# Modulation rows reordered, gate rows made on TensorE, and one chain for both inverses in a two-layer decoder kernel

## The chip, the cores and the metric

The kernel runs on one core of a Trainium2 chip. The metric is the device time of one execution in microseconds (us). The engines are TensorE (PE, its weight loads PEld), VectorE (DVE), ScalarE (ACT), GpSimd (POOL) and SyncE (SP), whose queue issues nearly all loads, in program order.

## The reference, cut to what matters

One sequence of 256 tokens of width 1024 goes through a first block and then a second block. The change lies in the first part of the first block.

```python
def hybrid_layer(x, c, w_ada, b_ada, ...):
    mods = jax.nn.silu(c) @ w_ada + b_ada
    shift1, scale1, gate1, shift2, scale2, gate2 = jnp.split(mods[:, None, :], 6, axis=-1)
    h = rms_norm(x, norm1_g) * (1.0 + scale1) + shift1
    proj = h @ w_in
    y_rwkv = rwkv7_time_mix(proj[..., :RWKV_PROJ], ...)
    y_moba = moba_attention(proj[..., RWKV_PROJ:], q_norm_g, k_norm_g)
    x = x + gate1 * (jnp.concatenate([y_rwkv, y_moba], axis=-1) @ w_out)
    h = rms_norm(x, norm2_g) * (1.0 + scale2) + shift2
    y = moe_ffn(h.reshape(B * S, D), w_router, b_router, w_gate_up, b_gate_up, w_down, b_down)
    return x + gate2 * y.reshape(B, S, D).astype(x.dtype)

def rwkv7_time_mix(p, ...):
    ...
    def step(state, inp):
        r_t, w_t, k_t, v_t, kk_t, a_t = inp
        sa = jnp.einsum('bhij,bhj->bhi', state, -kk_t)
        state = (state * w_t[:, :, None, :]
                 + sa[..., None] * (kk_t * a_t)[:, :, None, :]
                 + v_t[..., None] * k_t[:, :, None, :])
        y_t = jnp.einsum('bhij,bhj->bhi', state, r_t)
        return state, y_t
    ...
```

`mods` has 6 parts of 1024 columns. `rwkv7_time_mix` has 8 heads of width 64; `moba_attention` is causal attention of 8 heads here, since the sequence is one block long. `moe_ffn` has 32 experts, four for each token. The second block is a stick-breaking attention with 256 memory tokens, and a feed-forward part.

## The kernel before, in words

**Order of work.** Up to about 287 us the kernel makes the modulation, the projections, the time mix, the attention, w_out, and the router. From there to about 1200 us it streams the experts' weights, 6 chunks of 2 MB for each expert. The rest is the second block. Weights come through `stream` (L135, its DMA is L140): each call takes a slot of 2 MB and issues one load on SP. The ring has three slots, and two further places, lent[0] and lent[1], serve the first part as working memory (X and Y) and the experts as slots later. A load waits on SP until its slot is free, and all later loads wait behind it. The order of the instructions on each engine is not written by hand: the framework's scheduler sets it from the program's order and its own estimates.

**Modulation.** w_ada's columns are taken in 12 chunks of 512. `ada_rows` (L279) makes the rows of several chunks in one bank of PSUM: a matmul with the bias (L281), then for each chunk 8 matmuls of 128x512 (L286, 16 records in the trace), which leave four partial sums for each chunk, one in each quarter of the bank's partitions. ScalarE copies the bank (L292), and `ada_col` (L324) turns rows into columns. Chunks 0 and 2, then 1 and 3, are made at the start, chunks 6 to 9 (shift and scale of the second norm) after the attention's projections. The two gates (chunks 4, 5 and 10, 11) are made in `gate_rows` (L298): VectorE multiplies and accumulates in one operation (L306), POOL in two (L308, L310), over 8 pieces of each chunk, and `gate_bc` adds up the partitions and spreads the sum by a matmul with ones.

**Projections.** h is split in two parts, hh and hl, and each piece of a weight into wsh (ScalarE, L147) and wsl (L148, on VectorE, every fourth on POOL); a product is three matmuls. `dense_T` (L397 to L400, "pj") makes the lora's inputs, k, r and v in this order, `dense_N` (L412 to L414, "pn") the attention's q, k and v, which the texts call q, k2 and v2. The lora's second matrices are wua and gup; cb is a table of constants.

**Time mix.** The 256 tokens are two superchunks of 128. `sub` (L541) makes a triangular matrix for each head of a superchunk (lab), and its diagonal blocks of 16x16 (Lc, by lc). `invert` (L558) inverts these blocks in 15 steps: POOL makes a selection (sel, L566), TensorE a row (L567), VectorE multiplies by it and adds (L572, L574). The two superchunks' steps alternate. Then follow the transposes (tr, L660), decays (dc, L655), the masked products Lak, Lrk, Lrb (L671) and `solve` (L696) with Dt (the inverse spread out), f and u on TensorE. The attention's heads (L786 to L820) run between these: `s` is normalized on VectorE (L803). mqs (L601) is the normalized q or k, turned by mt (L609). sc2 and sh2 (L632, L633) are the second norm's scale and shift, with small loads of norm_g (L629) and of the router's weights (L628). prod (L641) is the product of r, k and r_k for the bonus.

Of the kernel before, what the change touches and what calls it, by code (L numbers as in the profile page):

```python
# [121 lines left out]
class Kernel:  # L122
# [132 lines left out]
    def phase1(self):  # L255
# [15 lines left out]
        bada = self.gate2[0:13, 512:1024]  # L271
        nc.sync.dma_start(bada[1:13], A["b_ada"])
# [6 lines left out]
        def ada_rows(cis):  # L279
            ps = self.psum("ada")  # L280
            PE.matmul(ps[0:32, :], ident[0:13, 1:33], bada, start=True, stop=False, skip_group_check=True)  # L281
            for n, i in enumerate(cis):
                w = self.stream(A["w_ada"][:, i * 512:(i + 1) * 512].rearrange("(k p) f -> p k f", p=128), 8, 512)
                for k in range(8):
                    j = k % 4
                    PE.matmul(ps[32 * j:32 * j + 32, :], scw[:, k, 32 - i:64 - i], w[:, k, :],  # L286
                              start=n == 0 and 0 < k < 4, stop=n == len(cis) - 1 and k >= 4, skip_group_check=True)
                if i == 0:
                    nc.sync.dma_start(x1, A["x"].rearrange("(a p) d -> p a d", p=128))
                    self.expert_bias(pxn)  # L290
            r = p1.tile([128, 512], F32, tag="ar", name="ar")
            ACT.activation(r, ps, AF.Copy)  # L292
            return r

        gacc = p1.tile([128, 4, 512], F32, tag="gacc", name="gacc")
        sc = scw[:, :, 32]

        def gate_rows():  # L298

            for q, i in enumerate((4, 5, 10, 11)):  # L300
                w = self.stream(A["w_ada"][:, i * 512:(i + 1) * 512].rearrange("(k p) f -> p k f", p=128), 8, 512)
                o, eng = gacc[:, q], POOL if q % 2 else DVE
                for k in range(8):
                    c = sc[:, k:k + 1]
                    if eng is DVE and k:
                        DVE.scalar_tensor_tensor(o, w[:, k], c, o, op0=OP.mult, op1=OP.add)  # L306
                    else:
                        eng.tensor_scalar(w[:, k] if k else o, w[:, k], c, None, op0=OP.mult)  # L308
                        if k:
                            eng.tensor_tensor(o, w[:, k], o, op=OP.add)  # L310
                r = slice(32 * q, 32 * q + 1)
                eng.tensor_tensor(o[r], o[r], self.gate2[r, 512:1024], op=OP.add)
# [18 lines left out]
        for q, i in enumerate((4, 5, 10, 11)):  # L331
            nc.gpsimd.dma_start(self.gate2[32 * q:32 * q + 1, 512:1024], A["b_ada"][i:i + 1])
# [23 lines left out]
        X, Y = lend(0), lend(1)  # L356
# [116 lines left out]
        self.act_set("natural_log_exp_and_others")  # L473

# [45 lines left out]
        eB, eC = ExitStack(), ExitStack()  # L520
        pb = self.pool("pb", es=eB)
        blk16, e16, idd = self.kb("blk16"), self.kb("e16"), self.kb("idd")
# [17 lines left out]
        def sub(s):  # L540

            tt = slice(s * 128, s * 128 + 128)
            L16 = pb.tile([128, 8, 128], F32, tag="L16", name="L16")
            Lof = pb.tile([128, 8, 128], F32, tag="Lof", name="Lof", bufs=2)
            for p, ps in pairs(aT, bT, tt, "lab"):
                DVE.tensor_tensor(par(L16, p), ps, bc("m16", 4), op=OP.mult)
                DVE.tensor_tensor(par(Lof, p), ps, bc("moff", 4), op=OP.mult)
            Lc = pb.tile([128, 8, 16], F32, tag=f"Lc{s}", name="Lc")
# [3 lines left out]
            ACT.activation(Lc.rearrange("p h q -> p (h q)"), ps[:, 0:128], AF.Copy)  # L552

            Tc = pb.tile([128, 8, 16], F32, tag=f"Tc{s}", name="Tc")
            POOL.tensor_copy(Tc, e16[:, None, :].to_broadcast([128, 8, 16]))
            return Lof, Lc, Tc

        def invert(s, r):  # L558

            Lof, Lc, Tc = parts[s]  # L560
            if r % 4 == 0:
                rows[s] = self.psum("row", chain=True)
                for q in range(r, min(r + 4, 15)):
                    if s == 0:
                        sel[q] = pb.tile([128, 128], F32, tag="sel", name="sel", bufs=5)
                        POOL.tensor_scalar(sel[q], blk16, e16[:, q:q + 1], None, op0=OP.mult)  # L566
                    PE.matmul(rows[s][:, (q % 4) * 128:(q % 4) * 128 + 128], sel[q], Lc.rearrange("p h q -> p (h q)"),  # L567
                              start=True, stop=True, skip_group_check=True)
            n = 15 - r
            t = pb.tile([128, 8, 16], F32, tag=f"tq{s}", name="tq")  # L570
            o = (r % 4) * 128
            DVE.tensor_tensor(t[:, :, 0:n], rows[s][:, o:o + 128].rearrange("p (h q) -> p h q", h=8)[:, :, r + 1:16],  # L572
                              Tc[:, :, r:r + 1].to_broadcast([128, 8, n]), op=OP.mult)
            DVE.tensor_tensor(Tc[:, :, r + 1:16], Tc[:, :, r + 1:16], t[:, :, 0:n], op=OP.add)  # L574

        parts = [sub(s) for s in range(2)]
        parts2, rows, sel = {}, {}, {}
        for r in range(15):
            for s in range(2):
                invert(s, r)  # L580
# [37 lines left out]
        r1 = ada_rows(range(6, 10))  # L618
        gate_rows()
# [20 lines left out]
        for m in range(4):  # L640
            DVE.scalar_tensor_tensor(prod[:, m], rT[:, m], self.v("rk", m), kT[:, m], op0=OP.mult, op1=OP.mult)  # L641
# [54 lines left out]
        def solve(s):  # L696
            Lof, Lc, Tc = parts[s]
# [3 lines left out]
            for hf in range(2):  # L701
                hsl = slice(4 * hf, 4 * hf + 4)
                (POOL if hf else DVE).tensor_tensor(
                    Dt[:, hsl], Tc[:, hsl, None, :].to_broadcast([128, 4, 8, 16]),
                    blk16.rearrange("p (b q) -> p b q", q=16)[:, None].to_broadcast([128, 4, 8, 16]), op=OP.mult)
# [186 lines left out]
        for dst, q in ((gate, 0), (self.gate2, 2)):  # L892
            for h in range(2):
                ACT.activation(dst[:, h * 512:(h + 1) * 512], gate_bc(q + h), AF.Copy)
# [733 lines left out]
```

## Time and profile before

| | |
|---|---|
| runs before, median of 3 | 1540.79 us (1537.72 to 1542.02) |
| the profiled execution | 1538.45 us |
| its span | 1536.7 us |
| TensorE busy | 1405.6 us (91%) |
| VectorE busy | 574.7 us (37%) |
| ScalarE busy | 387.6 us (25%) |
| POOL busy | 200.3 us (13%) |
| DMA of experts' weights on the chain that ended last | 24% of the span |
| granted TensorE clock, mean | 0.982 |

Busy shares are means over three stages with different limits, so what a change in one stage is worth has to be read in that stage. Times in the rows below are counted from the span's start. A row of a timeline shows the start, the length, the engine, the line and the operation, and in brackets how long the engine stood idle before and what ended that. The matmuls' ends are modelled, so that two in a row overlap by a little, and the spacing of their starts is the better measure.

### The profile page before, as it was taken

What the parts mean: (1) busy time and instruction counts of PE and PEld (TensorE: products, weight loads), DVE (VectorE), ACT (ScalarE), POOL (GpSimd) and SP (SyncE); (2) the same over time, 40 slices, a digit from 0 to 9 for tenths busy, and PEclk for the clock granted to TensorE, in tenths of its full rate; (3) what the DMA queues carried; (4) which work ended last, traced back from release to release, by engine and by line L of the source; (5) the groups of instructions that cost most, each with busy time, mean ns of one, the idle gap of its engine ahead of it and who ended that gap; (6) DMA issues with size and microseconds to landing.
All of it is one profiled execution on the core that took longest, in us unless ns stands there. A gap on an engine that the chain in (4) does not pass through costs nothing.

```text
span 1536.7 us, 19084 instructions
## 1 busy us (share of the span) xinstructions
PE 1405.6 (91%) x7818; PEld 805.5 (52%) x7818; DVE 574.7 (37%) x1138; ACT 387.6 (25%) x759; POOL 200.3 (13%) x180
## 2 busy tenths in 40 slices
PE   4999999899999999888988878999988899799997
PEld 1986776443434344233333334443333497599996
DVE  2576886422222222122112122121211446655455
ACT  4872244200100011011001011110100367355552
POOL 1233581000000000000000000000000334212221
PEclk9998999899999999999999999999999999999999
DMA  9833746899999999999999999999999851535440
GB/s 332 277 110 116 272 165 266 345 429 427 426 426 386 427 428 428 428 427 426 428 428 428 426 422 428 428 429 427 426 428 428 334 186 55 219 138 192 178 152 28
DMA packets 74885, 505.15 MB, mean 329 GB/s; under 512 B 5693, under 2 KB 6717, under 8 KB 50313
## 3 DMA queue, kind: packets, MB, share of 16 engines
q1 hardware_dynamic: 74328, 503.22, 80.3%
q8 instruction: 63, 1.03, 0.3%
q10 hardware_dynamic: 288, 0.52, 0.1%
q14 instruction: 30, 0.24, 0.0%
q0 software_dynamic: 176, 0.14, 0.0%
HBM read 502.82 MB, written 1.05 MB: 328 GB/s over the span
## 4 chain that ended last, share of the span: by engine, by line
PE 43%; DMA 24%; DVE 2%; ACT 1%; issue 0%; SPq 0%; DVEq 0%; ACTq 0%
DMA w<-w_gate_up 24%; PE py L116 7%; PE pg L116 6%; PE pu L116 6%; PE d L1302 3%; PE d L1301 3%; PE d L1303 3%; PE ga L116 2%; PE acc L1308 2%; PE acc L1309 2%; PE acc L1310 2%; PE cb L116 2%; ACT at L1169 1%; PE z L1389 0%; PE so L1419 0%
## 5 line engine op out<-in xcount | busy, mean ns | idle before, releaser
L116 PE MATMUL pg<-w,xe 128*64 128x512 f32 x1024 | 270.9, 599 | 43.5 <-DMA w<-w_gate_up 43.0
L116 PE MATMUL pu<-w,xe 128*64 128x512 f32 x1024 | 268.4, 594 | 0.0
L116 PE MATMUL py<-w,at 128*64 128x512 f32 x1024 | 228.9, 599 | 23.8 <-ACT at L1169 20.6
L1158 DVE TENSOR_SCALAR u<-pu 128x512 f32<-128x512 f32 (+1 forms) x33 | 22.2, 675 | 452.5 <-PE pu L116 439.2
L1157 ACT ACTIVATE sg<-pg 128x512 f32<-128x512 f32 (+1 forms) x33 | 19.3, 586 | 669.7 <-PE pg L116 668.0
L116 PEld LDWEIGHTS pg<-w,xe 128*64 128x64 f32 x1024 | 72.1, 137 | 190.2 <-issue 115.8
L116 PEld LDWEIGHTS py<-w,at 128*64 128x64 f32 x1024 | 71.1, 137 | 158.8 <-issue 130.3
L116 PEld LDWEIGHTS pu<-w,xe 128*64 128x64 f32 x1024 | 75.8, 137 | 145.7 <-issue 145.6
L147 ACT ACTIVATE w3h<-w 128x512 fp32r<-128x512 f32 x184 | 113.9, 629 | 100.5 <-PE d L1302 54.3
L148 DVE TENSOR_TENSOR w3l<-w,w3h 128x512 fp32r<-128x512 f32 x132 | 97.7, 751 | 102.0 <-ACT w3h L147 98.3
L148 POOL TENSOR_TENSOR w3l<-w,w3h 128x512 fp32r<-128x512 f32 x52 | 68.3, 1320 | 433.7 <-ACT w3h L147 426.4
L1182 DVE TENSOR_TENSOR y<-py,gate 64x512 f32<-64x512 f32 x64 | 44.1, 689 | 209.3 <-PE py L116 208.5
L1301 PE MATMUL d<-xh,w3h 128*128 128x256 f32 x352 | 99.8, 285 | 0.9 <-ACT xh L1287 0.9
L1302 PE MATMUL d<-xl,w3h 128*128 128x256 f32 x352 | 100.0, 284 | 0.5 <-DVE xl L1288 0.5
L1303 PE MATMUL d<-xh,w3l 128*128 128x256 f32 x352 | 99.7, 284 | 0.0
L1249 POOL TENSOR_TENSOR wml<-w,wml 128x512 fp32r<-128x512 f32 x4 | 5.1, 1276 | 682.5 <-ACT wml L1248 682.5
L116 PEld LDWEIGHTS ga<-s,xm 128*128 128x128 f32 x512 | 63.4, 201 | 13.5 <-issue 11.9
L1301 PEld LDWEIGHTS d<-xh,w3h 128*128 128x128 f32 x352 | 67.7, 193 | 1.6 <-ACT xh L1287 1.4
L1302 PEld LDWEIGHTS d<-xl,w3h 128*128 128x128 f32 x352 | 67.9, 193 | 0.9 <-DVE xl L1288 0.7
L1303 PEld LDWEIGHTS d<-xh,w3l 128*128 128x128 f32 x352 | 67.9, 193 | 0.0
L116 PE MATMUL ga<-s,xm 128*128 128x128 f32 x512 | 66.5, 289 | 1.2 <-DVE s L1108 1.2
L116 PE MATMUL cb<-y,swt 128*128 128x512 f32 x128 | 59.2, 605 | 0.8 <-DVE y L1182 0.8
(409 smaller groups left out, 2014.4 us busy)
## 6 DMA issues: line engine op xcount, KB each, us to landing
w<-w_gate_up SPq DMA_DIRECT2D x128, 2048.0 KB, 30.5
w<-w_down SPq DMA_DIRECT2D x71, 2048.0 KB, 28.3
w<-w_ada SPq DMA_DIRECT2D x12, 2048.0 KB, 9.5
w<-w_up SPq DMA_DIRECT2D x8, 2048.0 KB, 7.5
w<-w_in SPq DMA_DIRECT2D x6, 2048.0 KB, 12.5
w<-w_in_sb SPq DMA_DIRECT2D x5, 2048.0 KB, 16.8
w<-w_out SPq DMA_DIRECT2D x4, 2048.0 KB, 8.7
w<-w_mem_kv SPq DMA_DIRECT2D x1, 2048.0 KB
```

What stands on the lines that cost most here:

```text
L116: return self._keep(self.tc.nc.tensor.matmul(*a, **k))
L147: self.nc.scalar.activation(hi, src, AF.Copy)
L148: eng.tensor_tensor(lo, src, hi.bitcast(F32), op=OP.subtract)
L1157: ACT.activation(cut(s, c), cut(pg, c), AF.Sigmoid, scale=1.702)
L1158: DVE.tensor_scalar(cut(u, c), cut(pu, c), 8.0, -6.0, op0=OP.min, op1=OP.max)
L1182: DVE.tensor_tensor(st[e & ~1][2][r, hs], py[64 * h:64 * h + 64], self.gate2[64 * h:64 * h + 64, hs], op=OP.mult)
L1301: PE.matmul(o, wh[:, ws], xh[:, k], start=k == 0 and i % 2 == 0, stop=False, skip_group_check=True)
L1302: PE.matmul(o, wh[:, ws], xl[:, k], start=False, stop=False, skip_group_check=True)
L1303: PE.matmul(o, wl[:, ws], xh[:, k], start=False, stop=k == 7, skip_group_check=True)
L1308: PE.matmul(o, lh, rh, start=start, stop=False)
L1309: PE.matmul(o, ll, rh, start=False, stop=False)
L1310: PE.matmul(o, lh, rl, start=False, stop=stop)
```

## The change

- Chunks 6 to 9 are made right after v's projection, ahead of the attention's q. Their weights go by turns to lent[1] (chunks 6 and 8) and to the ring (7 and 9). Y takes lent[1] after that.
- The gates' chunks 4, 5, 10 and 11 are made by `ada_rows` on TensorE too, at the place in the program where all of these stood before. `gate_bc` picks and adds up the four partial sums of a row with a matmul by a selecting column. The four loads of b_ada on POOL's queue go.
- The 15 selections are made ahead, in 15 tiles, at the place in the program behind v's projection.
- Lc and Tc hold both superchunks. Each step's row is one matmul of 128x256, its two VectorE operations work on 16 blocks instead of 8, and there is one chain of 15 steps instead of two.
- prod is four scalings on ScalarE and one POOL multiplication instead of four VectorE operations.

```diff
@@ ada_rows
+        POOL.memset(bada[0:1], 0.0)
-        def ada_rows(cis):
-            ps = self.psum("ada")
+        def ada_rows(cis, tag="ar", pools=(None,), chain=False):
+            ps = self.psum("ada", chain=chain)
...
-                w = self.stream(A["w_ada"][:, i * 512:(i + 1) * 512].rearrange("(k p) f -> p k f", p=128), 8, 512)
+                w = self.stream(A["w_ada"][:, i * 512:(i + 1) * 512].rearrange("(k p) f -> p k f", p=128), 8, 512,
+                                pools[n % len(pools)])
...
-        def gate_rows():
...
-        def gate_bc(q):
+        def gate_bc(i):
             ps = self.psum("adab", chain=True)
-            PE.matmul(ps, self.k("ones"), gacc[:, q], start=True, stop=True)
+            PE.matmul(ps, self.k("sel32")[:, i:i + 1].to_broadcast([128, 128]), rg, start=True, stop=True)
...
-        X, Y = lend(0), lend(1)
+        X = lend(0)
@@ after k, r and v
+        r1 = ada_rows(range(6, 10), pools=(lent[1], None), chain=True)
+        Y = lend(1)
...
+        psel = self.pool("psel", es=eB)
+        sel = [psel.tile([128, 128], F32, tag=f"sel{q}", name="sel") for q in range(15)]
+        for q in range(15):
+            POOL.tensor_scalar(sel[q], blk16, e16[:, q:q + 1], None, op0=OP.mult)
@@ the inversion
+        Lc, Tc = (pb.tile([128, 2, 8, 16], F32, tag=n, name=n) for n in ("Lc", "Tc"))
+        POOL.tensor_copy(Tc.rearrange("p s h q -> p (s h) q"), e16[:, None, :].to_broadcast([128, 16, 16]))
+        def invert(r):
+            if r % 2 == 0:
+                rows[0] = self.psum("row", chain=True)
+                for q in range(r, min(r + 2, 15)):
+                    PE.matmul(rows[0][:, (q % 2) * 256:(q % 2) * 256 + 256], sel[q],
+                              Lc.rearrange("p s h q -> p (s h q)"), start=True, stop=True, skip_group_check=True)
             n = 15 - r
+            t = pb.tile([128, 16, 16], F32, tag="tq", name="tq")
+            o = (r % 2) * 256
+            T = Tc.rearrange("p s h q -> p (s h) q")
+            DVE.tensor_tensor(t[:, :, 0:n], rows[0][:, o:o + 256].rearrange("p (h q) -> p h q", h=16)[:, :, r + 1:16],
+                              T[:, :, r:r + 1].to_broadcast([128, 16, n]), op=OP.mult)
+            DVE.tensor_tensor(T[:, :, r + 1:16], T[:, :, r + 1:16], t[:, :, 0:n], op=OP.add)
...
         for r in range(15):
-            for s in range(2):
-                invert(s, r)
+            invert(r)
@@ after the attention's projections
-        r1 = ada_rows(range(6, 10))
-        gate_rows()
+        rg = ada_rows((4, 5, 10, 11), "ag")
...
         for m in range(4):
-            DVE.scalar_tensor_tensor(prod[:, m], rT[:, m], self.v("rk", m), kT[:, m], op0=OP.mult, op1=OP.mult)
+            ACT.activation(prod[:, m], rT[:, m], AF.Copy, scale=self.v("rk", m))
+        POOL.tensor_tensor(prod, prod, kT, op=OP.mult)
```

**SP, the loads of the first 100 us.** Each row is an instruction in SP's order, with its line, what it writes and reads, and how often it stands there in a row; w_in's 128x8x288 is the lora's, the others k, r, v and then the attention's. Before:

```order
L289 DMA x_65<-x 128x2x1024
L246 DMA bt<-b_gate_up 32x2048
L140 DMA w<-w_ada 128x8x512 x3
L140 DMA w<-w_in 128x8x288
L445 DMA cb<-cst_b 128x1616
L140 DMA w<-w_in 128x8x512 x3
L442 DMA wua<-rwkv_w_up 64x512
L443 DMA wua<-rwkv_a_up 64x512
L444 DMA gup<-rwkv_g_up 80x2x512
L140 DMA w<-w_in 128x8x512 x3
L140 DMA w<-w_ada 128x8x512 x8
```

And after:

```order
L291 DMA x_65<-x 128x2x1024
L246 DMA bt<-b_gate_up 32x2048
L140 DMA w<-w_ada 128x8x512 x4
L140 DMA w<-w_in 128x8x288
L423 DMA wua<-rwkv_w_up 64x512
L424 DMA wua<-rwkv_a_up 64x512
L425 DMA gup<-rwkv_g_up 80x2x512
L426 DMA cb<-cst_b 128x1616
L140 DMA w<-w_in 128x8x512 x3
L140 DMA w<-w_ada 128x8x512 x2
L140 DMA w<-w_in 128x8x512
L140 DMA w<-w_ada 128x8x512
L140 DMA w<-w_in 128x8x512 x2
L140 DMA w<-w_ada 128x8x512 x4
```

Of the four w_ada loads at the start, the third is chunk 6. The lora's small matrices stand ahead of cb and of k's weights. Chunks 7 and 9 come ahead of q's weights and chunk 8 behind them, and chunks 4, 5, 10 and 11 come last.

**POOL, the selections.** hl is the second part of h, wsl 128x288 a split of the lora's weights, wsl 128x512 one of k's or of later weights. After:

```order
L356 TENSOR_TENSOR hl<-hf,hh 128x256 x2
L148 TENSOR_TENSOR wsl<-w,wsh 128x288
L356 TENSOR_TENSOR hl<-hf,hh 128x256 x2
L463 TENSOR_SCALAR sel<-cb 128x128 x15
L148 TENSOR_TENSOR wsl<-w,wsh 128x288
L148 TENSOR_TENSOR wsl<-w,wsh 128x512 x3
```

Before, the selections stood behind all splits of r and v and of most later weights, the first five in one row and the rest between steps of the inversion. Now all 15 stand ahead of the lora's last split.

**VectorE, from the inversion's end to the masked products of superchunk 0.** Before:

```order
L574 TENSOR_TENSOR Tc<-Tc,tq 128x8 x2
L655 TENSOR_TENSOR dc<-lent,ge 128x128 x4
L308 TENSOR_SCALAR gacc<-w,gate_74 128x512
L306 SCALAR_TENSOR_TENSOR gacc<-w,gate_74,gacc 128x512
L671 TENSOR_TENSOR Lak<-lk,cb 128x4x128
L306 SCALAR_TENSOR_TENSOR gacc<-w,gate_74,gacc 128x512
L671 TENSOR_TENSOR Lak<-lk,cb 128x4x128
L655 TENSOR_TENSOR dc<-lent,ge 128x128 x4
L671 TENSOR_TENSOR Lrk<-lk,cb 128x4x128
```

And after:

```order
L559 TENSOR_TENSOR Tc<-Tc,tq 128x16
L638 TENSOR_TENSOR dc<-lent,ge 128x128 x4
L614 SCALAR_TENSOR_TENSOR sc_71<-adac,sc_71 128x8
L615 COPY sh_72<-adac 128x8
L654 TENSOR_TENSOR Lak<-lk,cb 128x4x128 x2
L638 TENSOR_TENSOR dc<-lent,ge 128x128 x4
L619 TENSOR_TENSOR W<-W,cv 128x32
L654 TENSOR_TENSOR Lrk<-lk,cb 128x4x128 x2
```

The gates' accumulations between these are gone. sc2's and sh2's operations (L614, L615), which stood behind superchunk 1's Lrb before, now stand ahead of superchunk 0's Lak.

## Rows read from the trace of the kernel before

**Rows 1.** Windows by stage: busy time of each engine, granted clock, DMA share, GB/s.

```profile
core 0: us, PE busy (x) PEld busy (x) DVE busy (x) ACT busy (x) POOL busy (x), PEclk, DMA share, GB/s
...
120.00:128.00 8.00, 6.34 (x23) 5.60 (x24) 7.04 (x19) 3.78 (x9) 4.12 (x5) 0.52 0.42 160
128.00:137.00 9.00, 9.00 (x39) 7.08 (x39) 4.80 (x14) 2.28 (x6) 0.00 (x0) 0.69 0.00 2
...
165.00:237.00 72.00, 68.65 (x734) 57.23 (x731) 59.58 (x118) 25.25 (x69) 52.57 (x36) 1.00 0.58 206
...
287.00:1190.00 903.00, 832.41 (x4008) 334.38 (x4006) 203.24 (x412) 78.14 (x159) 5.11 (x4) 0.99 1.00 423
```

**Rows 2.** TensorE's timeline, the first expert product.

```profile
286.87 1.03 PE L116 MATMUL pg<-w,xe 128*64 128x512 f32 x4
```

**Rows 3.** TensorE's waits from 0 to 165 us: total, times, longest.

```profile
PE ada L286 <- DMA w<-w_ada: 14.2, 3, 6.5
...
PE mt L609 <- DVE mqs L601: 3.3, 1, 3.3
PE pn L414 <- DVE wsl L148: 2.4, 1, 2.4
```

**Rows 4.** A window (columns as in rows 1), and ScalarE's timeline at k's weights.

```profile
38.00:47.00 9.00, 8.96 (x75) 8.72 (x75) 7.40 (x14) 6.37 (x18) 4.14 (x7) 1.00 1.05 385
...
45.27 2.20 ACT L147 ACTIVATE wsh<-w 128x512 fp32r<-128x512 f32 x4 [2.63 <-DMA w<-w_in]
```

**Rows 5.** TensorE's timeline, chunks 0 and 3 of w_ada.

```profile
13.55 3.64 PE L286 MATMUL ada<-w,gate 128*32 128x512 f32 x16 [6.50 <-DMA w<-w_ada]
...
34.49 1.93 PE L286 MATMUL ada<-w,gate 128*32 128x512 f32 x16 [1.29 <-DMA w<-w_ada]
```

**Rows 6.** The selections (ns min/median/max), and POOL's timeline at a lora split.

```profile
L566 POOL TENSOR_SCALAR sel<-cb x15: 600/640/1034, 118.4 to 156.7; 128x128 f32<-128x128 f32 x15
...
42.41 0.95 POOL L148 TENSOR_TENSOR wsl<-w,wsh 128x288 fp32r<-128x288 f32 x1 [0.38 <-ACT wsh L147]
```

**Rows 7.** SP's timeline at k2's and v2's loads, and TensorE's at q's first product.

```profile
66.91 18.90 SPq L140 DMA_DIRECT2D w<-w_in  x2
...
90.72 0.80 PE L412 MATMUL pn<-wsh,hh 128*128 128x512 f32 x1
```

**Rows 8.** TensorE's timeline, products of k2 and of v2.

```profile
116.20 0.39 PE L413 MATMUL pn<-wsh,hl 128*128 128x512 f32 x1
116.43 0.39 PE L412 MATMUL pn<-wsh,hh 128*128 128x512 f32 x1
...
126.39 0.63 PE L413 MATMUL pn<-wsh,hl 128*128 128x512 f32 x1
126.82 0.63 PE L414 MATMUL pn<-wsl,hh 128*128 128x512 f32 x1
```

**Rows 9.** VectorE's timeline at the inversion and first Lak, TensorE's at the first transposes.

```profile
142.75 0.28 DVE L572 TENSOR_TENSOR tq<-row,Tc 128x120 f32<-128x120 f32 x1 [3.54 <-PE row L567]
...
163.44 0.30 DVE L574 TENSOR_TENSOR Tc<-Tc,tq 128x8 f32<-128x8 f32 x2
...
167.91 0.69 DVE L671 TENSOR_TENSOR Lak<-lk,cb 128x512 f32<-128x512 f32 x1
...
164.25 0.66 PE L660 MATMUL tr<-ca,vT 128*128 128x128 f32 x4
```

**Rows 10.** Lines by form, 0 to 300 us: busy us, mean ns; then the normalizing multiplies.

```profile
L306 DVE SCALAR_TENSOR_TENSOR gacc<-w,gate,gacc 128x512 f32<-128x512 f32 x14 | 12.6, 898 | 0.2
...
L567 PE MATMUL row<-Lc,sel 128*128 128x128 f32 x60 | 8.7, 286 | 0.0
...
L803 DVE TENSOR_SCALAR s<-s,st x16: 340/795/1382, 195.5 to 226.1; 128x128 f32<-128x128 f32 x8, 128x256 f32<-128x256 f32 x8
```

**Rows 11.** SP's timeline, the last w_ada loads, and VectorE's at sc2's operation.

```profile
151.44 26.24 SPq L140 DMA_DIRECT2D w<-w_ada  x5
...
188.60 0.17 DVE L632 SCALAR_TENSOR_TENSOR sc<-adac,sc 128x8 f32<-128x8 f32 x1 [1.24 <-DMA sc<-norm_g]
```

More of the change, by code (lines that the diff above doesn't have):

```diff
@@ L290, in ada_rows @@
                     self.expert_bias(pxn)
-            r = p1.tile([128, 512], F32, tag="ar", name="ar")
+            r = p1.tile([128, 512], F32, tag=tag, name="ar")
             ACT.activation(r, ps, AF.Copy)
             return r
-        gacc = p1.tile([128, 4, 512], F32, tag="gacc", name="gacc")
-        sc = scw[:, :, 32]
-        def gate_rows():
[L300 to L312, printed above, removed]
-        def gate_bc(q):
+        def gate_bc(i):
             ps = self.psum("adab", chain=True)
-            PE.matmul(ps, self.k("ones"), gacc[:, q], start=True, stop=True)
+            PE.matmul(ps, self.k("sel32")[:, i:i + 1].to_broadcast([128, 128]), rg, start=True, stop=True)
             return ps
@@ L330, in phase1 @@
         ss = p1.tile([128, 2], F32, tag="ss", name="ss")
-        for q, i in enumerate((4, 5, 10, 11)):
-            nc.gpsimd.dma_start(self.gate2[32 * q:32 * q + 1, 512:1024], A["b_ada"][i:i + 1])
         ra = ada_rows((0, 2))
@@ L471, in phase1 @@
                     lambda i, ps, m, dst=dst, mi=mi: shift_mix(dst[:, i], ps, m, mi + i))
+        r1 = ada_rows(range(6, 10), pools=(lent[1], None), chain=True)
+        Y = lend(1)
         eA.close()
         self.act_set("natural_log_exp_and_others")
+        blk16, e16, idd = self.kb("blk16"), self.kb("e16"), self.kb("idd")
+        eB, eC = ExitStack(), ExitStack()
+        psel = self.pool("psel", es=eB)
+        sel = [psel.tile([128, 128], F32, tag=f"sel{q}", name="sel") for q in range(15)]
+        for q in range(15):
+            POOL.tensor_scalar(sel[q], blk16, e16[:, q:q + 1], None, op0=OP.mult)
         PB, BM = self.kb("blk"), self.kb("blkm")
@@ L547, in sub @@
                 DVE.tensor_tensor(par(Lof, p), ps, bc("moff", 4), op=OP.mult)
-            Lc = pb.tile([128, 8, 16], F32, tag=f"Lc{s}", name="Lc")
             ps = self.psum("lc", chain=True)
@@ L551, in sub @@
                 PE.matmul(ps[:, h * 16:(h + 1) * 16], L16[:, h], e16, start=True, stop=True, skip_group_check=True)
[L552 to L568, printed above, removed]
-            n = 15 - r
[L570 to L574, printed above, removed]
@@ L576, in phase1 @@
-        parts = [sub(s) for s in range(2)]
-        parts2, rows, sel = {}, {}, {}
+            ACT.activation(Lc[:, s].rearrange("p h q -> p (h q)"), ps[:, 0:128], AF.Copy)
+            return Lof
+        Lc, Tc = (pb.tile([128, 2, 8, 16], F32, tag=n, name=n) for n in ("Lc", "Tc"))
[6 more added lines that the diff above has]
+                              Lc.rearrange("p s h q -> p (s h q)"), start=True, stop=True, skip_group_check=True)
+            n = 15 - r
+            t = pb.tile([128, 16, 16], F32, tag="tq", name="tq")
[4 more added lines that the diff above has]
+            DVE.tensor_tensor(T[:, :, r + 1:16], T[:, :, r + 1:16], t[:, :, 0:n], op=OP.add)
@@ L578, in phase1 @@
+        parts, parts2, rows = [sub(s) for s in range(2)], {}, {}
         for r in range(15):
-            for s in range(2):
-                invert(s, r)
+            invert(r)
         qn, kn2 = Y[:, 0], Y[:, 1]
@@ L696, in solve @@
         def solve(s):
-            Lof, Lc, Tc = parts[s]
+            Lof, Ts = parts[s], Tc[:, s]
             nb, R, Lrb = parts2[s]
@@ L703, in solve @@
                 (POOL if hf else DVE).tensor_tensor(
-                    Dt[:, hsl], Tc[:, hsl, None, :].to_broadcast([128, 4, 8, 16]),
+                    Dt[:, hsl], Ts[:, hsl, None, :].to_broadcast([128, 4, 8, 16]),
                     blk16.rearrange("p (b q) -> p b q", q=16)[:, None].to_broadcast([128, 4, 8, 16]), op=OP.mult)
@@ L891, in phase1 @@
         w_out((4, 5, 6, 7))
-        for dst, q in ((gate, 0), (self.gate2, 2)):
+        for dst, i in ((gate, 4), (self.gate2, 10)):
             for h in range(2):
-                ACT.activation(dst[:, h * 512:(h + 1) * 512], gate_bc(q + h), AF.Copy)
+                ACT.activation(dst[:, h * 512:(h + 1) * 512], gate_bc(i + h), AF.Copy)
         eN.close()
```

2 lines of the change are left out of this document (removed).

## The prediction

> **What bounds the kernel now.** I read the windows by stage first. From 287 to 1190 us the DMA share is 1.00 [rows 1]: there the experts' weights set the pace. The first product of an expert's weights starts at 286.87 [rows 2], and from there on the change touches no line. A slot of that stage comes free only when a product has used it, so I carry an earlier or later end of the first part over one to one. The question is thus only what happens between 0 and 286.87. In that part I read TensorE's timeline and its waits. TensorE waits for w_ada three times, 14.2 us in all, once for mqs (3.3) and once for a split of a weight (2.4) [rows 3]; elsewhere it is busy nearly throughout (68.65 of 72 us from 165 to 237 [rows 1]). So I add up TensorE's path, and look at each queue only where it makes TensorE wait. The sum is against the profiled execution, 1538.45 us; the median of the runs before is 1540.79, 2.3 above it, and the final number is set on the median. A difference under 0.3% (4.6 us) can't be told from none.
>
> **The start.** The load of chunk 6 now stands on SP's queue between those of chunks 1 and 3, because its place in lent[1] is free at once. While DMA is saturated the core gets 385 GB/s [rows 4]; 2.097 MB more ahead of chunk 3 and of everything behind it is 5.4 us. TensorE's wait for chunk 3, 1.3 us before, grows to 6.7. After such waits (6.50 us) the same 16 matmuls took 3.64 us, against 1.93 right after other work [rows 5]; I take the slow price, +1.7. The three small loads of the lora's second matrices (0.59 MB, 1.5 us by the same rate) now come ahead of k's weights, which landed at 45.27 with ScalarE waiting 2.63 us for them [rows 4]; TensorE has the lora's products until then, so I count 0.6. Together **+7.7**, bounds 5.5 and 9.5.
>
> **The selections.** POOL makes all 15 right after the first splits of hh, behind cb's load and ahead of the lora's last split. One took 640 ns in the median, 1034 at most [rows 6]. cb's load came ahead of the lora's small matrices before and comes behind them now; at 385 GB/s it lands about 47, the 15 end about 56.5, and the lora's last split (0.95 us [rows 6]) about 57.4. TensorE's order has some forty products of k ahead of its use, and k's splits start at 45.27 + 7.7 = 53, so I take TensorE to come there at about 58. I count 0, covered by k's products; with 1034 ns each the cover is gone and it is +6. The Trainium skill, "SBUF — State Buffer", section "Who interferes with whom", speaks against this place: a VectorE operation with two operands in SBUF and a GpSimd operation that reads SBUF exclude each other for a whole instruction. The trace has such pairs, the normalizing multiplies beside POOL's gate work, with 795 ns in the median where the shortest took 340 [rows 10], so the rule can't be set aside. By the rule, six of k's splits on VectorE would each come up to 0.64 us later, an estimate of 3.8 us, of which TensorE would see what its queue of ready pieces doesn't cover; the sum stays, and the bound of 6 covers it.
>
> **Rows 6 to 9.** Their 64 matmuls (four times 1.93 us [rows 5], plus the bias) move from 148 to 164 us to between v and k2: no net work. What moves with them is the loading. q's weights now wait for the slot of v's weights, issued before at 66.91 plus 18.90 us [rows 7], so about 93 with the shift of the start, and land about 101. Before, q's first product ran at 90.72 [rows 7], which would be 98.4; chunks 6 and 7 stand ahead of q in TensorE's order and fill 4.3 us. I count 0, bound +3.
>
> **Gates' rows on TensorE.** Four more times 1.93 us and a bias of 0.5: **+8.2**, of which 6.2 stand ahead of the transposes of superchunk 0, and 2.0 behind them. Nothing hides them, TensorE being the busy engine. Off VectorE go 14 accumulations (12.6 us [rows 10]) and two starts, off POOL about 29 us of the same.
>
> **The stretch from 118 to 139.** The wait for mqs (3.3) and that for the split (2.4) [rows 3] go when chunks 8 and 9 and the first superchunk's products stand there. After the wait for mqs the granted clock was 0.52, then 0.69 [rows 1], and the products of v2 came at 0.43 us instead of 0.23 [rows 8]; 8 us at 0.52 and 9 at 0.69 lose 6.6, of which I take 6. Together **-11.7**; bounds 0 (the wait comes back elsewhere) and -12.3.
>
> **The inversion.** Before, its first and last VectorE operations were at 142.75 and 163.44 [rows 9], 60 small operations with waits for TensorE's rows between them. Now there are 30 of twice the width. The first took 0.28 us for 120 elements [rows 9]; at once to twice that, 30 take 8 to 17 us, beside TensorE's products and ended before Lak, and nothing needs them before Dt, behind Lak: nothing on the path. TensorE's part shrinks from 60 records (8.7 us busy [rows 10]) to 30 wider ones, -0.9; of the turns between rows and chunks I take another -1.5 (bounds 0 and -3). Up to the transposes: 7.7 + 6.2 - 11.7 - 0.9 - 1.5 = **-0.2**, so they start at 164.0 instead of 164.25 [rows 9].
>
> **The new wait.** VectorE's order now has sc2's operation (L614) ahead of the first Lak; it stood behind Lrb of superchunk 1 before. It needs small loads that stand on SP's queue behind the load of chunk 11. Before, that was issued at 177.3 (151.44 plus 26.24, less one issue) and sc2 was ready at 188.60 [rows 11]: 11.3 us. Chunk 11 now takes the slot that chunk 4's matmuls leave, about 155, so sc2 is ready about 166.5. Queued behind it on VectorE: Lak, dc, Lrk, Lrb and with them all of superchunk 0. Lak ran at 167.91 [rows 9] and by the sum above would run at 167.7: **0**, but any further gain ahead of it would be eaten. Bound +3.
>
> **Behind Lak.** TensorE has chunk 11 (+2.0) and no attention heads beside the second solve (+1, one VectorE step between its products). Against that VectorE loses 14 us of gate work in a stretch where it was busy 59.58 of 72 [rows 1], and the multiplies beside POOL's gate work (16, each some 0.45 us above the shortest [rows 10]) another 7. prod's four operations go to ScalarE and POOL, which have room. How much of that TensorE was paying can't be read from its busy time, whose ends are modelled. Bounds: 0, and -10, half of the 21 us, as about half of these operations stood between products of one superchunk that feed each other. I take -5, the middle, since no row is nearer to either end. Sum: -0.2 + 0 + 2.0 + 1.0 - 5.0 = **-2.2**; 1540.79 - 2.2 is 1538.6.
>
> **Rivals.**
> *The freed VectorE pays in full.* All 10 us behind Lak come, and the early part shifts by only 5.5: -2.2 - 5 - 2.2 = -9.4, **1531**; with every bound on the good side, -14, 1527. For it: the two solves alternate between VectorE and TensorE, and VectorE had gate work between their operations. Against it: the new wait before Lak.
> *TensorE's clock and added work are not paid back.* The start's longer wait (+7.7) and gates on TensorE (+8.2) stay, but the -11.7 does not come: mqs's operations are still made by VectorE between splits and inversion, and if TensorE again stands still over some 3 us there, the products of v2 again run at half pitch. It decides if mqs is late, that is if a PE wait of over 2 us shows ahead of mt. Price: 7.7 + 8.2 - 2.4 - 0.5 - 4 = +9, **1550**; half of it, +4.5, 1545. For it: two idle stretches are added, none of those before is certain to go. Against it: chunks 8 and 9 give VectorE 4 us more ahead of mqs.
> *The loads set Lak.* Chunk 11 is issued late and sc2 keeps Lak at 168 or later, whatever is saved ahead: 0 to +3, **1541**.
>
> **How the numbers follow.** The forecast has 0.46, with its bounds -8 and +6: faster 0.14, same 0.26, slower 0.06. The first rival has 0.27, all faster; the second 0.21, all slower; the third 0.06, same. That makes faster 0.41, same 0.32, slower 0.27. The range reaches from the good rival's far end, 1527, to the bad one's, 1550.
>
> **What would show it.** Right: chunk 3's matmuls near 40 us and at 3.6 us for 16; the first expert product within 4 us of 286.87; no wait for mqs; a granted clock of 1.0 from 118 to 139; sc2's operation waiting for DMA near 166. Wrong: a POOL wait in front of the lora's last products; a granted clock of half between 100 and 165; a first expert product before 280 or after 293; any difference behind it that the first product's time does not explain.

## The result and the profile after

The changed kernel takes **1555.86 us** in the median of 4 runs (1554.04 to 1558.21), the kernel before 1539.39 in 4 runs on the same chip. The ratio is 1.0114, with a 95% interval from 1.0096 to 1.0132: slower, and above the forecast range of 1527 to 1550. The profiled execution took 1558.21 us, its span is 1556.4.

The first expert product now runs at 306.65 us, 19.8 later than in [rows 2], and the span is 19.7 us longer. All of it was thus lost ahead of the experts, as the prediction had assumed. TensorE's timeline of the changed kernel at that product:

```profile
306.65 1.03 PE L116 MATMUL pg<-w,xe 128*64 128x512 f32 x4
```

A table of landmarks, from TensorE's timelines of both kernels, shows where:

| first or last instruction | before | after | later by |
|---|---|---|---|
| first product of the lora | 38.23 | 48.18 | 10.0 |
| last product of v | 90.14 | 103.81 | 13.7 |
| first transposes | 164.25 | 180.19 | 15.9 |
| first product of w_out | 237.66 | 255.89 | 18.2 |
| first expert product | 286.87 | 306.65 | 19.8 |

Two thirds are lost before v is done. TensorE's timeline of the changed kernel at chunks 1 and 3, which answers to [rows 5], then its wait in k's products, and a wait that comes later, ahead of lab:

```profile
30.58 1.92 PE L288 MATMUL ada<-w,gate 128*32 128x512 f32 x16
39.22 3.64 PE L288 MATMUL ada<-w,gate 128*32 128x512 f32 x16 [6.71 <-DMA w<-w_ada]
46.45 1.87 PE L307 MATMUL adac<-ca,ar 128*128 128x4 f32 x8 [3.59 <-ACT ar L294]
48.18 0.56 PE L378 MATMUL pj<-hh,wsh 128*128 128x256 f32 x1
...
64.55 0.38 PE L381 MATMUL pj<-hh,wsl 128*128 128x256 f32 x1 [2.08 <-POOL wsl L148]
...
136.50 1.14 PE L524 MATMUL lab<-lent 64*128 64x128 f32 x8 [2.85 <-DVE lent L504]
```

The same columns in the kernel before:

```profile
37.13 1.05 PE L324 MATMUL adac<-ca,ar 128*128 128x4 f32 x8 [0.72 <-ACT ar L292]
```

Chunk 3 comes 4.7 us later and at the slow rate, as forecast. What was not forecast is the row below it: the columns wait 3.59 us for ScalarE's copy of the rows. ScalarE's and GpSimd's timelines show why:

```profile
44.15 1.77 ACT L147 ACTIVATE wsh<-w 128x288 fp32r<-128x288 f32 x5 [11.34 <-DMA w<-w_in]
45.83 0.57 ACT L294 ACTIVATE ar<-ada 128x512 f32<-128x512 f32 x1
```

```profile
51.21 1.65 POOL L356 TENSOR_TENSOR hl<-hf,hh 128x256 fp32r<-128x256 f32 x2 [4.75 <-ACT hh L355]
52.97 10.78 POOL L463 TENSOR_SCALAR sel<-cb 128x128 f32<-128x128 f32 x15
63.71 2.02 POOL L148 TENSOR_TENSOR wsl<-w,wsh 128x288 fp32r<-128x288 f32 x2
```

In the changed kernel ScalarE's copy stands behind five splits of the lora's weights, and those wait until 44.15 for their load. The selections end at 63.7 and only then does GpSimd make the lora's last split.

Further on, windows of the changed kernel (columns as in [rows 1]; the first two the stretch where v2 starts, the last from the first transposes to w_out) and VectorE's wait for sc2, ahead of Lak:

```profile
144.00:148.00 4.00, 4.00 (x34) 3.46 (x32) 3.93 (x11) 0.46 (x3) 0.64 (x1) 0.86 0.91 348
148.00:152.00 4.00, 3.91 (x12) 2.96 (x11) 3.47 (x7) 3.25 (x7) 0.00 (x0) 0.50 0.02 4
...
180.19:255.89 75.70, 72.07 (x748) 58.97 (x748) 39.51 (x101) 26.16 (x71) 3.72 (x4) 0.98 0.43 153
```

```profile
185.72 0.17 DVE L614 SCALAR_TENSOR_TENSOR sc<-adac,sc 128x8 f32<-128x8 f32 x1 [3.10 <-DMA sc<-norm_g]
185.88 1.28 DVE L654 TENSOR_TENSOR Lak<-lk,cb 128x512 f32<-128x512 f32 x2
```

The same stretch before, the window ahead of w_out's first product:

```profile
164.25:237.66 73.41, 69.40 (x742) 58.01 (x739) 60.24 (x119) 26.51 (x71) 52.57 (x36) 1.00 0.58 210
```

VectorE lost 21 of 60 us and GpSimd 49 of 53, and TensorE's stretch is not shorter but 2.3 us longer.

### The profile page after: what moved, and what is told of

The parts are those of the page before. It is cut to its first block, busy times and chain, and to the rows that moved or that the text cites. A ratio compares the mean times of both kernels' runs of the same rounds, so it can differ in the third digit from the quotient of the medians.

```text
span 1556.4 us, 19046 instructions
## 1 busy us (share of the span) xinstructions
PE 1419.0 (91%) x7854; PEld 811.6 (52%) x7854; DVE 549.6 (35%) x1086; ACT 390.9 (25%) x765; POOL 151.2 (10%) x145
## 3 DMA queue, kind: packets, MB, share of 16 engines
HBM read 502.81 MB, written 1.05 MB: 324 GB/s over the span
## 4 chain that ended last, share of the span: by engine, by line
PE 42%; DMA 24%; DVE 2%; ACT 1%; issue 0%; SPq 0%; DVEq 0%; ACTq 0%
DMA w<-w_gate_up 24%; PE py L116 7%; PE pg L116 6%; PE pu L116 6%; PE d L1285 3%; PE d L1284 3%; PE d L1286 3%; PE ga L116 2%; PE acc L1291 2%; PE acc L1293 2%; PE acc L1292 2%; PE cb L116 2%; ACT at L1152 1%; PE z L1372 0%; PE so L1402 0%
## 5 line engine op out<-in xcount | busy, mean ns | idle before, releaser
L1141 DVE TENSOR_SCALAR u<-pu 128x512 f32<-128x512 f32 (+1 forms) x33 | 22.2, 675 | 452.9 <-PE pu L116 439.5
```

The costliest lines, as they stand in the source:

```text
L1141: DVE.tensor_scalar(cut(u, c), cut(pu, c), 8.0, -6.0, op0=OP.min, op1=OP.max)
```

## The experiments

Medians stand beside that of the kernel before, 1538.5 to 1540.2 in the runs on the same chip; "changed" is 1555.9, measured on a chip where before took 1539.4. Theory A blames placement at the start, theory B the work added on TensorE. The edits are cut to what matters.

**Undoing one part.**

```diff
# hold6: in stream, ahead of the load of chunk 6 into its place t
+            self.nc.gpsimd.tensor_copy(t[:, 0:1], hold)
...
-        r1 = ada_rows(range(6, 10), pools=(lent[1], None), chain=True)
+        r1 = ada_rows(range(6, 10), pools=(lent[1], None), chain=True, hold=hh[:, 7, 0:1].bitcast(F32))
```

> The changed kernel, but chunk 6's load into lent[1] has to wait until the last piece of hh is made (one GpSimd copy of a column into its place ahead of the load). Theory A, the start: the +10 us at the lora's first product (38.2 before, 48.2 after) come from this load and from the ScalarE order that goes with it (the copy of chunks 1 and 3's rows behind five splits of the lora's weights), and they carry over to the end one to one. Then the lora's first product is back at 38 to 40 us, the first expert product near 297 instead of 306.7, and the time about 1546. Theory B, the added TensorE work: the four gate chunks (8 us) and a granted clock that falls again later set the end, and early delays are taken up by later waits. Then the lora starts early again but the first expert product stays above 303 and the time above 1552.

1543.9 us, ratio 1.0021 [0.9978, 1.0065]: **12 us back**. The lora starts at 39.53, ScalarE's copy stands ahead of the splits again, the first expert product is at 296.30. Theory A holds.

```diff
# sel_late: the same lines, moved behind the pool of the inversion
-        psel = self.pool("psel", es=eB)
...
         pb = self.pool("pb", es=eB)
+        sel = [pb.tile([128, 128], F32, tag=f"sel{q}", name="sel") for q in range(15)]
```

> The changed kernel, but the 15 selections are made in the pool that opens for the inversion, so that they come on GpSimd behind the splits of r and v. Theory A: the wait of 2.1 us for GpSimd's split of the lora's weights goes, and with it the waits of ScalarE's splits for their buffers; v's last product comes 2 to 4 us earlier than 104.0, the time is 1552 to 1554. Theory B: TensorE finds other waits, the time stays at 1555 to 1557.

1550.7, 5.2 less than changed: the wait for GpSimd's split is gone, and v's last product comes 2.0 us earlier. The total is a little more than expected.

```diff
# r1_back
-        r1 = ada_rows(range(6, 10), pools=(lent[1], None), chain=True)
...
+        r1 = ada_rows(range(6, 10))
         rg = ada_rows((4, 5, 10, 11), "ag")
```

> The changed kernel, but chunks 6 to 9 are made again at their old place, ahead of the gates' chunks and all through the ring; so no load stands in lent[1] at the start. Theory A: the start is as before, 10 us come back, less what the later place of these chunks costs: 1544 to 1549. Theory B: 1553 to 1558, as the early place of chunks 6 to 9 was worth as much as the start cost.

1552.2, between the two theories and near B's. The lora starts at 39.88, so the start is mended here too, but 8 us less come back than in hold6: TensorE waits 2.6 us for lab's input and 4.5 for mqs, and the granted clock is at half from 123 to 133. So in that setting the early place of these chunks is worth 8 us.

```diff
# gates_dve: gate_rows and gate_bc of the kernel before; in invert
+                    sel[q] = pb.tile([128, 128], F32, tag="sel", name="sel", bufs=5)
```

> The changed kernel, but the gates' rows are accumulated on VectorE and GpSimd as before, and (for want of room) the selections are made in 5 buffers between the steps of the one chain. Theory A: the start keeps its +10; the gates' 8 us on TensorE go, but VectorE's 14 us come back between the products of the time mix: 0 to -4 against the change, beside the 2 to 4 us of the selections, so 1549 to 1554. Theory B: the full 8 us and more come off, 1545 to 1547.

1558.5, *slower* than changed by 2.6, where both theories had it faster. The stretch from the first transposes to w_out takes 79.1 us here and 75.7 in the changed kernel; the granted clock is at half from 178 to 191.

**Two or three fixes together.**

```diff
# hold_late: hold6 and sel_late; hold_late_small: also
+        POOL.tensor_copy(wua[:, 0:1], hh[:, 7, 0:1].bitcast(F32))
+        POOL.tensor_copy(gup[:, 0, 0:1], hh[0:80, 7, 0:1].bitcast(F32))
...
+            nc.sync.dma_start(self.cb, A["cst_b"])
             nc.sync.dma_start(wua[0:64], A["rwkv_w_up"])
```

> The changed kernel with both: chunk 6's load held until hh's last piece, and the selections made in the inversion's pool. Theory A (two losses at the start, in different places, that carry over one to one): 12 us and 5 us come off the changed kernel's 1556, less some 2 that the two share; 1539 to 1542, level with the kernel before. Theory C (the selections only cost time because the start was late and VectorE and GpSimd were crowded): nothing more than the held load gives, 1543 to 1545.

1543.5, ratio 1.0022 [1.0011, 1.0033]: theory C, the selections cost no more once the start is on time. TensorE waits 1.7 and 1.1 us for the lora's second products (lo) and 1.6 for a split, waits that the kernel before did not have.

> The run with held load and late selections (1543.5), and also the small loads of the lora's second matrices held until hh's last piece, with cb's load ahead of them, so that SP's order and the place of lo on TensorE are those of the kernel before. Theory A: v's last product comes back from 96.6 to 92, 3 to 5 us earlier, and carries over: 1538 to 1541, level with the kernel before. If TensorE had only waited there instead of elsewhere: 1542 to 1545.

1541.6, ratio 1.0011 [1.0000, 1.0023], just above the first expectation. In the profiled execution v ends at 90.66, the first transposes are at 163.24, the first expert product is at 286.64, all within 1 us of before; it is the fastest of the 12 runs, 3.3 us under their median. With three placements mended, everything else that the change does costs at most 0.23%.

**One part alone, on the kernel before.** These runs had the surprise.

```diff
# chain_only: Lc, Tc and invert of the change, selections in 5 buffers
# gates_only: rg and gate_bc of the change, gate_rows left out
# r1_early, r1_early_held: chunks 6 to 9 behind v, without and with the hold of hold6
# prod_only: the scalings and the multiplication of the change
```

> The kernel before with only the inversion changed: one chain over both superchunks, selections in 5 buffers between its steps; rows 6 to 9, gates and prod as before. Theory A: the chain lies beside TensorE's work and is no part of the path, within 3 us of before, 1536 to 1542. Theory D: the chain makes superchunk 0 wait for superchunk 1's inverse and lengthens the stretch behind the transposes, 73 us before and 76 to 77 in the changed kernels: 1541 to 1545.

1554.5: neither. The first transposes are at 164.65, as before, and yet 15 us are lost behind them. Windows of chain_only, then of chain_fill, which is told below:

```profile
162.00:180.00 18.00, 17.11 (x176) 13.12 (x172) 13.76 (x33) 6.29 (x12) 6.78 (x4) 1.00 0.87 322
180.00:195.00 15.00, 14.05 (x100) 12.30 (x100) 12.81 (x23) 1.79 (x3) 15.00 (x9) 0.59 0.51 159
195.00:210.00 15.00, 15.00 (x69) 13.93 (x68) 4.25 (x14) 5.21 (x16) 12.42 (x10) 0.50 0.40 142
```

```profile
162.00:180.00 18.00, 17.69 (x173) 13.11 (x172) 15.29 (x35) 5.80 (x11) 7.32 (x4) 1.00 0.83 291
180.00:195.00 15.00, 14.09 (x134) 12.18 (x133) 11.49 (x22) 3.09 (x6) 15.00 (x10) 1.00 0.61 208
195.00:210.00 15.00, 14.17 (x94) 10.94 (x93) 12.08 (x25) 6.03 (x20) 14.75 (x12) 1.00 0.58 215
```

In chain_only TensorE's granted clock (PEclk) is at half from 183 to 210 us. Ahead of the fall stands one wait. It is shown for chain_only and then for the kernel before, which kept the clock at 1.00:

```profile
180.95 0.30 PE L657 MATMUL tr<-ca,dc 128*128 128x128 f32 x1 [1.85 <-DVE dc L652]
```

```profile
178.35 0.30 PE L660 MATMUL tr<-ca,dc 128*128 128x128 f32 x1 [1.58 <-DVE dc L655]
```

VectorE's timeline of the kernel before tells what that wait is made of: dc stands behind the gates' accumulations.

```profile
173.64 3.64 DVE L306 SCALAR_TENSOR_TENSOR gacc<-w,gate,gacc 128x512 f32<-128x512 f32 x4
177.32 0.68 DVE L312 TENSOR_TENSOR gacc<-gacc,gate 1x512 f32<-1x512 f32 x1
177.93 0.88 DVE L655 TENSOR_TENSOR dc<-lent,ge 128x128 f32<-128x128 f32 x4
```

With the gates on TensorE the longest wait for dc is 0.4 to 0.5 us (changed, hold6, hold_late, r1_back, gates_only).

> The kernel before with only the gates' rows on TensorE (and the shorter p1 pool that follows). Theory A: 8 us of products against 14 us less on VectorE and 29 less on GpSimd: 1539 to 1545, of which some 4 us are new waits of TensorE for the lora's second products (lo), whose small matrices now come early. Theory B (the added TensorE work is the whole of the change's loss): 1548 and more.

1549.5, ratio 1.0070 [1.0052, 1.0088]: in theory B's range and above A's, though 10 us is not the whole of the change's loss. Of the 7.7 us by which the first expert product comes later in the profile, 3.0 are there at v's end, where TensorE waits for a split and for lo as in hold_late. The clock stays at 1.00 behind the transposes. There all four gate chunks, 7.7 us of products, stand behind the first transposes, and the stretch to w_out is 4.8 us longer than before: so VectorE's relief gave some 2.9 us back.

> The kernel before with one part of the change: chunks 6 to 9 right behind v, by turns in lent[1] and the ring, and with chunk 6's load held until hh's last piece. Gates, selections, both chains and prod as before. Theory A: the early place is worth what it was worth between the runs with the held load and with these chunks moved back (1543.9 and 1552.2), some 8 us, or at least the wait for mqs (3.3 us) and half the slow clock behind it; 1531 to 1536, faster than the kernel before. Theory E: that gain exists only when gates are on TensorE and VectorE is free; here VectorE's gate work moves into the gap, 1538 to 1542.

1556.8: theory E in direction, but far worse: the clock is at half from 163 to 201 us. hold_two_chains has the same early chunks and chains, but gates on TensorE and the changed prod:

> The changed kernel with chunk 6's load held, and with the two alternating chains of the kernel before and selections in 5 buffers; gates on TensorE, rows 6 to 9 early, prod changed. Theory A: like the run with held load and late selections, 1538 to 1542. Theory D: the stretch from the first transposes to w_out's first product shrinks from 77 to 74 us, 1536 to 1538.

1552.8, missed by both. Between 160 and 210 us the granted clock is 0.97 on the mean where r1_early_held has 0.62, and the kernel is 4 us faster with 8 us more of products on TensorE; that it is the gates and not prod that keep the clock is not shown apart, but likely, since prod alone lost it (below). Against hold_late (1543.5) two chains, with their selections in 5 buffers, cost 9 us with gates on TensorE, 4 of them ahead of the first transposes (173.09 against 169.08).

> The same part of the change alone, without the hold: chunk 6's load stands between those of chunks 1 and 3 and ScalarE's copy of rows 1 and 3 behind five splits, as in the change. Theory A: 8 to 12 us more than with the hold, lora's first product at 47 to 48 us. If the loss at the start is taken up later: within 3 us of the held one.

1567.6, 11 us more than with the hold; the lora's first product is at 46.00, 8.2 later, and the first transposes 6.9 later. This is the start's loss, seen on the other kernel; the rest shows behind the transposes, where the clock is at half for 44 us instead of 38.

> The kernel before with only prod changed: four scalings on ScalarE and one GpSimd multiplication, instead of four VectorE operations, two of which stood right ahead of mqs's chain on VectorE (2.0 us at 116 us). Theory F: mqs comes some 2 us earlier, TensorE's wait for it shrinks from 3.3 to about 1 us and with it the slow clock from 120 to 138 (6.8 us lost); 1531 to 1537. Theory A (parts that lie beside TensorE's work move nothing): 1538 to 1541.

The runs lie between 1537.7 and 1553.2, median 1548.1, ratio 1.0041 [1.0017, 1.0066]: as fast as before at one end, and 13 us slower at the other. The profiled one has the clock at half from 178 to 205, again behind the wait for dc, 1.76 us here. TensorE's wait for mqs grew (6.2 us), so theory F fell.

**The load or the order at the start.**

```diff
# copy_dve: the rows of chunks 1 and 3
+            if copy is DVE:
+                DVE.tensor_copy(r, ps)
# copy_first: ahead of the first split of the lora's weights
+            self.nc.scalar.activation(hi[:, 0:1], self.first, AF.Copy)
```

> The changed kernel with chunk 6's load left at the start, but the rows of chunks 1 and 3 are copied out of PSUM by VectorE instead of ScalarE, so that the copy does not stand behind ScalarE's splits of the lora's weights. It tells what of the start's 10 us is the load and what the order. If the order holds 3.6 us of it: TensorE's columns (adac) follow the rows within 1 us, the lora's first product is at 44 to 45 instead of 48.2, the time 1550 to 1553. If the copy waits on VectorE behind a split of the lora's weights as it did on ScalarE, the lora's first product stays at 47 to 48 and the time at 1554 to 1557.

1553.3, but the columns still waited 3.7 us, now for VectorE's copy behind a split, and the lora started at 49.27: the second case, its start a little later and its time a little below what was said.

> The changed kernel with chunk 6's load at the start, but the first split of the lora's weights has to wait for the copy of chunks 1 and 3's rows (a copy of one column into its output), so that ScalarE's order is the old one. It tells the load from the order. The load alone: chunk 3's products stay at 39 us, the columns follow within 1 us, the lora's first product at 44 to 45, 3 to 5 us off the changed kernel's 1556. If the order is harmless, the lora's first product stays at 47 to 49 since the lora's weights land at 44 anyway, and the time at 1554 to 1557.

The columns follow within 0.7 us, and the lora still starts at 46.65: ScalarE's first split waits for its load there until 44.83. So 8.4 of the 10 us are the load itself, which the lora's weights stand behind, and 1.5 the order. The total, 1572.5, says nothing on this: later orders changed too (5.3 us of new waits for ScalarE at one place).

**Is it the clock?**

```diff
# chain_fill, behind the transposes of a, superchunk 1; results not read
+                    for m in range(3):
+                        PE.matmul(ps, nat["v"][:, 0:128], nat["v"], start=True, stop=True)
```

> The run with only the chain changed (1554.5), plus three matmuls of 128x512 on the copied v of superchunk 1, whose result nothing reads; they stand on TensorE between the transposes and the decayed ones (dc), where it waited 1.85 us and behind which the clock fell to 0.5 from 182 to 210 us. If the wait sets the clock: the granted clock stays at 1.0 there, 12 to 15 us come back less at most 2 for the products, 1540 to 1544. If the fall comes from what the engine does otherwise in that stretch: it falls again, 1554 to 1558.

Median 1547.6, between the two expectations: four of six runs from 1543.6 to 1548.0 and two at 1557. In the profiled one, 1545.3, the wait is 0.63 us and the clock stays at 1.00 (windows above). The stretch from the first transposes to w_out takes 80.5 us there, with some 3 us of idle products in it, 86.5 in chain_only and 73.4 before. So the full clock is worth about 9 us of chain_only's 13 in that stretch; the other 4 us are lost at full clock too, and no run tells to what. Three idle matmuls don't bring the gain in each run.

> The kernel before plus idle matmuls of 128x512 whose result nothing reads: three in TensorE's wait for mqs (118 to 122 us) and one behind each rank product (276 to 280 us). If the waits set the clock: it stays near 1.0 from 120 to 138 and from 276 to 284, where 6.8 and 3.4 us were lost, 6 to 10 us faster than the kernel before, 1530 to 1534. If not: 1539 to 1543, the products' own time on top.

1555.1. The first part came out: the clock is full from 120 to 138, the first transposes are at 157.74, 6.5 us ahead of before. Then VectorE's dc came 2.79 us late instead of 1.58, and the clock was at half from 177 to 194. two_fills put idle matmuls there as well (expected 1533 to 1537; 1545 to 1555 if the gates on VectorE cost the clock in another place): 1554.6, with the clock at half from 185 to 209. There dc waited for the one buffer that the transposes behind the idle products read, and on VectorE it stood behind a gate operation that waited 3.51 us for its load; TensorE's wait for it came to 2.79 us again. In the place of mqs the idle products did not hold the clock this time, 0.74 from 118 to 138 us. small_fill (one idle matmul behind each rank product, expected 1538 to 1540) gave 1542.2, no gain over hold_late_small. No kernel of the study beats the one before.

## Why the prediction was wrong

By the profiles, forecast and measured part as follows:

| stretch | forecast | measured |
|---|---|---|
| up to the lora's first product | +7.7 | +10.0 |
| from there to the last product of v | 0 | +3.7 |
| from there to the first transposes | -7.9 | +2.3 |
| from there to the first expert product | -2.0 | +3.8 |

Three of the signs that the prediction named for being wrong came: a wait for GpSimd ahead of the lora's last products, a clock of half between 100 and 165 us, a first expert product after 293.

**The start: +7.7 forecast, 10.0 measured.** The mechanism was right (hold6 gives 12 us back), and chunk 3's wait and rate came as said, 6.71 and 3.64 us. The step that failed is a term left out, the columns between chunk 3 and the lora: they waited 3.59 us for ScalarE instead of 0.72 and took 1.87 instead of 1.05. The lora's own weights stood behind the same load, and ScalarE's order turned behind it. The orders read ahead of the prediction are those of SP, GpSimd and VectorE; ScalarE's was not among them.

**The selections: 0 forecast; +3.7 up to v's end, and 5 in sel_late's total.** The step that failed is the cover, "I count 0, covered by k's products". Its time of 57.4 for the lora's last split counted from cb's load at about 47; but the pieces of hl, which stand ahead of the selections, came at 51.2 with the late columns, the 15 took 10.8 us instead of 9.6, and the split started at 63.7. TensorE waited 2.1 us for it; another 1.5 are the half clock that ran on to 51.2 under the lora's products. The bound of +6 held it. With the start on time the cost is gone (hold_late). The exclusion of VectorE's splits that the prediction took into that bound did not show on VectorE: six of k's splits beside the selections took 0.69 to 0.85 us, those without them in sel_late 0.69 to 0.71. On GpSimd single selections took up to 1.08 us, against 0.60 in the median.

**The stretch from 118 to 139: -11.7 forecast.** This is the largest miss. The wait for mqs went, but a wait for VectorE's input of lab, the triangular matrix (2.85 us), took its place, and the clock fell twice, at 136 and at 147 us. The second of these, half clock from 147 to 153, stands behind no wait at all: TensorE was busy for 4.00 of the 4 us from 144 with small products. From v's end to the first transposes, waits and lost clock come to some 12 us before and 9 after, so some 3 of the 11.7 came. This was the second rival in part: a stand of some 3 us and a slow clock behind it came, but its own sign, a wait ahead of mt, did not. That its +9 lies nearer to the result than the forecast is in part luck: it had no more for the start, the columns and the selections than the forecast had. In hold_late_small the clock is 1.00 from 120 to 152 us, where it was 0.79 before: with the order at the start mended, the gain is there.

**Gates on TensorE: +8.2 forecast.** The four chunks took what was said: chunk 11's 16 matmuls are 1.92 us. The run that undid it was not faster: with gates on VectorE the clock fell again in the same stretch, as in most kernels with gates there.

**Behind Lak: -5 forecast for the freed VectorE, nothing measured.** The step "I take -5, the middle" failed. VectorE's busy time in the stretch fell from 60.2 to 39.5 us and the multiplies from 795 to 342 ns in the median; TensorE's waits for VectorE were 2.7 us before, and only those could be won, and 1.9 us of the 2.3 by which the stretch grew are chunk 11. The profile had said so: a bound engine with few waits gains little from a neighbour's relief, 2.9 us at most in gates_only. By the Trainium skill, "SBUF — State Buffer", section "Who interferes with whom", a tensor_scalar on VectorE, which the multiplies are, can contend with GpSimd; the trace agrees (342 ns with GpSimd's work gone), and it bought no time. The prediction had taken them for operations with two operands in SBUF; they read one tensor and a column of scalars. Another 1.5 us came between w_out and the first expert product, where the clock was 0.87 instead of 0.93.

**The new wait** is there (3.10 us ahead of Lak), and it hides behind TensorE's products, which show no wait for Lak.

**What stays open.** Which activity makes the clock fall is not settled. Behind the transposes a wait for dc of 1.58 us did not bring a fall (before), while 1.76 (prod_only), 1.85 (chain_only) and 2.79 (before_fill, two_fills) did; but the falls at 147 us in the changed kernel, at 176 in hold6 and at 172 in small_fill have no wait above 0.4 us in the 5 us ahead of them, and runs of one kernel differ.

## What to carry to other kernels

When a load may start early because its place happens to be free, ask what it now stands ahead of on its queue, and read every engine's order for what turned with it; holding it back by one small dependency gave back 12 of 16 us. Relief for an engine that the bound engine hardly waits for was worth little here, however much of it there was. Two single parts of this change took 8 and 15 us more by themselves (prod_only, chain_only), with half clock behind a wait that had grown by 0.2 to 0.3 us in their profiles, so look at the granted clock stretch by stretch before believing any other cause.

## What the runs showed that was not expected

The granted clock decides much between kernels whose work is the same. From 160 to 215 us the profiled executions lost, reckoned as the time at half clock halved, 13.6 us (chain_only), 18.8 (r1_early_held), 22.2 (r1_early), 13.6 (prod_only), 6.8 (gates_dve), 8.5 (before_fill) and 12.0 (two_fills), all with gates on VectorE and GpSimd, and at most 1.7 in the changed kernel, hold6, hold_late, r1_back, gates_only and hold_two_chains, all with gates on TensorE. The kernel before and chain_fill, with gates on VectorE, lost nothing there in their profiles; before, too, took 1553.2 us once in 87 runs, at a mean clock of 0.968 where its others had 0.977 to 0.986. The reckoning is an upper bound: chain_fill's full clock gave back 9 of chain_only's 13.6. Idle products in a wait held the clock in two profiles and not in a third, and no kernel with them was faster than the one before.
